# The second block's context weights move from SyncE's DMA queue to GpSimd's

## The chip, the cores and the metric

The kernel runs on one core of a Trainium2 chip. The metric is the device time of one execution in microseconds (us). The kernel before was timed three times; its time is the median of these runs.

## The reference

Two transformer blocks are computed in float32 for 512 latent tokens of width 1024; a sequence of 256 context tokens goes with each block. What matters here, cut short:

```
def reference(x, ..., ctx_2, ...):
    x = first_block(x, ...)      # differential attention + gated linear attention,
                                 # then 32 experts (2 per token, hidden width 512)
    return second_block(x, c_2, ctx_2, ...)   # DEPTH_2 = 2 layers

def second_block(x, c, ctx, ...):
    for i in range(2):
        last = i == 1
        hc = modulate(rms_norm(ctx), ...);  pc = hc @ w_in[i]   # context path
        k_na_c, v_na_c, k_mla_c, v_mla_c = ...                  # keys and values from pc
        h = modulate(rms_norm(x), ...);     p = h @ w_in[i]     # latent path
        y_na  = neighbourhood_attention(q, k, v, k_na_c, v_na_c, bias)
        y_gm  = spatial_gating(...)
        y_mla = dense_attention(q, [k_mla_c, k], [v_mla_c, v])
        x = x + g1 * merge_branches(y_na, y_gm, y_mla, gates, ...)
        x = x + g2 * (square(relu(h2 @ ffn_w1[i])) @ ffn_w2[i])
        if not last:  # the same three branches, merge and MLP for the context
            ctx = ctx + ...
    return x
```

The context path of layer 0 depends on nothing that the first block computes. In layer 1 it only makes keys and values.

## The kernel before

**Precision and weights.** Large products are made of three matmuls: each operand is split into a high part (fp32r) and a low part, and high by high, high by low and low by high are added up in PSUM (`mm3`, lines 188 to 194). Weights come from HBM as float32 in pieces of 128x1024 (512 KB). `load_split` (line 176) takes a `raw` buffer, loads a piece with `load` (line 151), and splits it with `split`: ScalarE writes the high part `wh` (line 168), VectorE the low part `wl` (line 169). There are four `raw` buffers and six `hl` buffers for the parts. A chunk of 256 output columns over a depth of 1024 is two pieces, so the raw buffers hold two chunks.

**Queues.** Every `load` is issued on SyncE (SP, line 152): the context's and the latent path's pieces (`wr`), the experts' weights (`we`, 384 pieces of 512 KB into 14 `wa` buffers, line 973), modulation weights and constants. GpSimd (POOL) issues the stores of results to HBM, the reading back of stored keys and values, the indirect gathers (token rows `xb` for the experts, line 979; expert results `yr`, line 1053) and the stores of expert results `Yd` (line 1041). It also computes: `acc` sums of `merge` (line 1732), sums of squares in `stat` (line 241), zeroing of `xb` (line 978).

**Order.** `weave` (line 79) writes the program out by the streams' planned times: the context path of layer 0, `path(0, 256)`, goes between the steps of the first block's output projection, routing, experts and combination (`run`, lines 401 to 411). Its MLP falls into the second half of the experts. The context path of layer 1, `path(1, 256)`, is woven into the MLP of layer 0's latent path (`self.fill`). That program order gives priorities; a planner then fixes each engine's queue when the kernel is built, taking what it holds ready, by priority. At run time every engine, SP and POOL too, takes its queue strictly in order: an instruction that waits holds all that stands behind it.

Experts go by in 16 pairs. A pair is 32 instructions each for gate and up (`gu`, line 1019) and 32 for down (`py`, line 1038), and its results go from PSUM to `yb` (ScalarE line 165, VectorE line 986) and by POOL to `Yd`.

Of the kernel before, what the change touches and what calls it, by code (L numbers as in the profile page):

```python
# [104 lines left out]
class Gen:  # L105
# [67 lines left out]
        self.nc.scalar.activation(hi, ps, AF.Copy, scale=g)  # L173
        self.nc.vector.scalar_tensor_tensor(lo, ps, g, hi.bitcast(F32), op0=OP.mult, op1=OP.subtract)

    def load_split(self, src, width):

        out = []
        total = src.shape[-1]
        for o in range(0, total, 1024):  # L180
            m = min(1024, total - o)
            raw = self.load(self.H.get("raw", self.nm("wr"))[:, :m], src[:, o:o + m])
            hi, lo = (self.H.get("hl", self.nm("w" + c), F32R)[:, :m] for c in "hl")
            self.split(hi, lo, raw)
            out += [(hi[:, j:j + width], lo[:, j:j + width]) for j in range(0, m, width)]
        return out
# [991 lines left out]
    def path(self, L, n, side=None, before=None):  # L1178
        nc, A = self.nc, self.A
        T = n // P  # L1180
        lat = n == 512
        kv_only = L == 1 and not lat
        src = self.xs_dram[L] if lat else (A["ctx2T"], self.xctx_dram)[L]
        dst = (self.xs_dram[1], self.out)[L] if lat else self.xctx_dram
        W = A["w_in2"][L]
        m = self.gains(L, 0 if lat else 1, 1)
# [17 lines left out]
        d = self.ctx_dram[L]  # L1204

        def row_tiles(chunk, evac, cols=256):
            w = self.load_split(W[chunk], 256)
            for t in range(T):
                ps = self.mm()
                self.rows(ps[:, :cols], h, t, [(x[:, :cols], y[:, :cols]) for x, y in w])  # L1210
                evac(t, ps[:, :cols])
                yield 2.6 if t == T - 1 else -2.6
# [30 lines left out]
        raw = yield from heads64(0, "k")  # L1243
# [48 lines left out]
        raw = yield from heads64(6, "q")  # L1292
# [57 lines left out]
        X = self.load_x(src, n, "xr")  # L1350
        ss = []
        for c in range(4):
            w = self.load_split(A["w_out2"][L, c], 256)
            for j in range(2):
                ps = self.mm()
                self.colsT(ps[:, :n], w, j, mg)
                i = 2 * c + j
                nc.vector.scalar_tensor_tensor(X[i], ps[:, :n], m["g1"][:, i:i + 1], X[i], op0=OP.mult, op1=OP.add)
                self.stat(ss, i, X[i], n)
                yield (5.1 if j else -5.1) * w1  # L1360
# [9 lines left out]
    def mlp(self, L, n, X, h2, g2, dst):  # L1370

        nc, A = self.nc, self.A
        w1, follow = n / 512, n == 512 and L == 0
        for q in range(4):
            u = self.pairs(8, n, "u")
            for c in range(4):
                w = self.load_split(A["ffn_w1"][L, q * 4 + c], 256)
                for j in range(2):
                    ps = self.mm()
                    self.colsT(ps[:, :n], w, j, h2)  # L1380
                    t = self.t2("uu")[:, :n]
                    nc.scalar.activation(t, ps[:, :n], AF.Relu)
                    nc.vector.tensor_tensor(t, t, t, op=OP.mult)
                    self.split(*u[2 * c + j], t)
                    yield (5.1 if j else -5.1) * w1
            if q == 3 and follow:
                ss = []
            for c in range(4):
                w = self.load_split(A["ffn_w2"][L, q, c], 256)
                for j in range(2):  # L1390
                    ps = self.mm()
                    self.colsT(ps[:, :n], w, j, u)
                    i = 2 * c + j
                    nc.vector.scalar_tensor_tensor(X[i], ps[:, :n], g2[:, i:i + 1], X[i], op0=OP.mult, op1=OP.add)
                    if q == 3:
                        nc.gpsimd.dma_start(dst[i], X[i])
                        if follow:
                            self.stat(ss, i, X[i], n)
                    yield (5.1 if j else -5.1) * w1
        if follow:  # L1400
            self.X, self.ss = X, ss
# [132 lines left out]
    def latent_attention(self, L, n, low, column, y):  # L1534
# [20 lines left out]

        for half in range(2):

            wkv = self.load_split(A["mla_w_ukv"][L, half], 512)
            KQ = [self.at("mkq") if lat else self.t2("mkr") for _ in range(T)]
            KR, VR = [x[:, :384] for x in KQ], self.many(T, 256, "mvr")  # L1560
            for t in range(T):
# [21 lines left out]
                    nc.gpsimd.dma_start(vc[t], d["vml"][t][:, half * 256:(half + 1) * 256])  # L1583
                vs = VR + vc
            if not kv_only:
                wq = self.load_split(A["mla_w_uq"][L, half], 384)
                QR = [KQ[t][:, 384:] if lat else self.t2("mqr") for t in range(T)]
                for t in range(T):
                    if t % 2 == 0:
                        room = self.dd("q")  # L1590
                    ps = room[:, t % 2 * 512:t % 2 * 512 + 384]
                    self.rows(ps, cq, t, wq)
                    self.copy_act(QR[t][:, :384], ps)
                yield 1
                r = rms(QR, 96)
                yield 1
                for t in range(T):
                    x = QR[t][:, :384].rearrange("p (h c) -> p h c", h=4)
                    tt(x, x, r[:, t][:, :, None].to_broadcast([P, 4, 96]), op=OP.mult)
                    x = x[:, :, 64:]  # L1600
                    if not lat:
                        tt(x, x, gq[:, 64:][:, None, :].to_broadcast([P, 4, 32]), op=OP.mult)
                        continue

                    tmp = self.t2("rp")
                    u, v = (tmp[:, i * P:(i + 1) * P].rearrange("p (h c) -> p h c", h=4) for i in range(2))
                    for o, z in ((u, rc), (v, rs)):
                        tt(o, x, z[:, t * 32:t * 32 + 32][:, None, :].to_broadcast([P, 4, 32]), op=OP.mult)
                    x, u, v = (z.rearrange("p h (a i c) -> p h a i c", a=2, i=2) for z in (x, u, v))
                    tt(x[:, :, :, 0], u[:, :, :, 0], v[:, :, :, 1], op=OP.subtract)  # L1610
                    tt(x[:, :, :, 1], u[:, :, :, 1], v[:, :, :, 0], op=OP.add)
                    yield 0.5
# [53 lines left out]
    def gating(self, L, n, h, W, row_tiles):  # L1666

        nc, A = self.nc, self.A
        T = n // P
        lng, lnb, ws, bs = (self.load(self.t2(x), A[x][L]) for x in ("gm_ln_g", "gm_ln_b", "gm_w_s", "gm_b_s"))  # L1670
        gv = [self.t2("gv") for _ in range(T)]
        sums = self.small(2 * T, "gsum")
        for c in range(2):
            def evac(t, ps):
                nc.scalar.activation(gv[t][:, c * 256:(c + 1) * 256], ps, AF.Gelu, accum_out=sums[:, c * T + t:c * T + t + 1])
            yield from row_tiles(8 + c, evac)
        mu, va = self.small(T, "gmu"), self.small(T, "gvs")
        nc.vector.tensor_tensor(mu, sums[:, :T], sums[:, T:], op=OP.add)
        nc.vector.tensor_scalar(mu, mu, -1.0 / 512, None, op0=OP.mult)
        for t in range(T):  # L1680
            sq = self.t2("sq")
            nc.scalar.activation(sq, gv[t], AF.Square, bias=mu[:, t:t + 1], accum_out=va[:, t:t + 1])
        rs = self.rsqrt(va, T, 1.0 / 512)
        for t in range(T):
            nc.vector.tensor_scalar(gv[t], gv[t], mu[:, t:t + 1], rs[:, t:t + 1], op0=OP.add, op1=OP.mult)
            nc.vector.tensor_tensor(gv[t], gv[t], lng, op=OP.mult)
            nc.vector.tensor_tensor(gv[t], gv[t], lnb, op=OP.add)
        u = self.many(4, n, "gu")
        for c in range(2):
            w = self.load_split(W[10 + c], 256)  # L1690
            for j in range(2):
                ps = self.mm()
                self.colsT(ps[:, :n], w, j, h)
                nc.scalar.activation(u[2 * c + j], ps[:, :n], AF.Gelu)
                yield (5.1 if j else -5.1) * T / 4
        y = self.pairs(4, n, "ygm")
        for g in range(4):
            ps = self.tp("gs")
            for t in range(T):
                nc.tensor.matmul(ps[:, t * P:(t + 1) * P], gv[t][:, g * P:(g + 1) * P], ws[:, g * P:(g + 1) * P], start=True, stop=True)  # L1700
            x = self.t2("gx")[:, :n]
            nc.vector.tensor_tensor(x.rearrange("p (t c) -> p t c", t=T), ps[:, :n].rearrange("p (t c) -> p t c", t=T),
                                    bs[:, g * P:(g + 1) * P][:, None, :].to_broadcast([P, T, P]), op=OP.add)
            nc.vector.tensor_tensor(x, x, u[g], op=OP.mult)
            self.split(*y[g], x)
        yield 1
        return y

    def merge(self, L, n, h, W, b, y, acc):
# [1 line left out]
        nc, A = self.nc, self.A  # L1711
        wo = A[("na_w_o", "gm_w_o", "mla_w_o")[b]][L]
        for c in range(4):
            w = self.load_split(W[12 + b * 4 + c], 256)
            th = []
            for j in range(2):
                ps = self.mm("pg")
# [3 lines left out]
                yield (5.1 if j else -5.1) * n / 512  # L1721
            if callable(y):
                y = y()
            w = self.load_split(wo[c], 256)
            for j in range(2):
                i = 2 * c + j
                ps = self.mm("pp")
# [170 lines left out]
```

## Time and profile before

| | us |
|---|---|
| median of three runs | 3545.32 |
| lowest and highest | 3538.56, 3549.27 |
| the profiled execution, its own time | 3544.75 |
| its span in the trace | 3542.7 |
| granted TensorE clock, mean share of full speed | 0.973 |

The span runs from the first to the last instruction in the trace; the profiled execution's own time is 2.05 us longer. Times in rows are counted from the span's start. PE is TensorE's matmuls, PEld its weight loads, DVE VectorE, ACT ScalarE, POOL GpSimd; SPq is the queue in which SyncE issues. A matmul's end is modelled, so a busy PE isn't one at its peak.

### The profile page before, as it was taken

To read this page: it belongs to the slowest core of one execution; us is meant where nothing else is said; L and a number is where in the kernel's file an instruction comes from. 1 tells how busy PE (TensorE), PEld (TensorE's weight loads), DVE (VectorE), ACT (ScalarE), POOL (GpSimd) and SP (SyncE) were. 2 spreads that over 40 slices of the span, in tenths; PEclk is the share of its full clock that TensorE was granted. 3 is DMA by queue.
4 is the path that set the end of the run, shared out by engine and by line. 5 is a ranking of instruction groups with operands and counts; after the bars stand their busy time and mean duration, and the time that the engine had idled before them with its cause. 6 is when DMAs were issued, how large, how long until landed. Compare 5 with 4: busy or idle time off the path is not lost. (4 is left out here: it accounts for less than half of the span.)

```text
span 3542.7 us, 48935 instructions
## 1 busy us (share of the span) xinstructions
PE 3357.0 (95%) x19280; PEld 2533.0 (71%) x19280; DVE 1693.2 (48%) x3173; ACT 1234.2 (35%) x2194; POOL 340.3 (10%) x410
## 2 busy tenths in 40 slices
PE   7999998999999999699999999999999999999999
PEld 4987546665666666497577777888797777778887
DVE  5336545435333333454347755444654466644443
ACT  4214314334322322233344433333334444423222
POOL 1000011012111100400001011000300001020000
PEclk9999999999999999799999999999999999999999
DMA  7241567898899898534642132333433221132332
GB/s 262 88 128 36 189 213 259 317 360 329 309 358 352 305 358 320 205 92 137 226 144 68 56 98 96 106 117 114 152 96 105 78 71 59 49 113 86 100 99 79
DMA packets 197459, 596.03 MB, mean 168 GB/s; under 512 B 32123, under 2 KB 36987, under 8 KB 197228
## 3 DMA queue, kind: packets, MB, share of 16 engines
q1 hardware_dynamic: 178460, 539.65, 43.8%
q0 software_dynamic: 18768, 53.24, 4.2%
q8 instruction: 152, 2.49, 0.3%
q14 instruction: 79, 0.65, 0.1%
HBM read 563.69 MB, written 33.29 MB: 169 GB/s over the span
## 5 line engine op out<-in xcount | busy, mean ns | idle before, releaser
L169 DVE TENSOR_TENSOR wl<-wr,wh 128x1024 fp32r<-128x1024 f32 (+2 forms) x452 | 553.0, 1229 | 534.3 <-ACT wh L168 504.6
L168 ACT ACTIVATE wh<-wr 128x1024 fp32r<-128x1024 f32 (+2 forms) x452 | 471.1, 1047 | 697.5 <-PE mm L193 489.8
L192 PE MATMUL mm<-wh,h 128*128 128x256 f32 (+1 forms) x1104 | 322.5, 292 | 6.3 <-ACT h L277 4.6
L193 PE MATMUL mm<-wl,h 128*128 128x256 f32 (+1 forms) x1104 | 318.8, 289 | 0.0
L194 PE MATMUL mm<-wh,h 128*128 128x256 f32 (+1 forms) x1104 | 318.0, 289 | 0.3 <-DVE h L278 0.2
L192 PE MATMUL mm<-u,wh 128*128 128x512 f32 (+1 forms) x768 | 276.6, 361 | 10.8 <-ACT wh L168 10.8
L192 PE MATMUL mm<-f,wh 128*128 128x512 f32 (+1 forms) x768 | 275.2, 361 | 8.6 <-ACT wh L168 5.0
L194 PE MATMUL mm<-u,wl 128*128 128x512 f32 (+1 forms) x768 | 274.3, 359 | 2.9 <-DVE wl L169 2.9
L193 PE MATMUL mm<-f,wh 128*128 128x512 f32 (+1 forms) x768 | 274.3, 358 | 0.0
L194 PE MATMUL mm<-f,wl 128*128 128x512 f32 (+1 forms) x768 | 273.3, 358 | 1.0 <-DVE wl L169 1.0
L193 PE MATMUL mm<-u,wh 128*128 128x512 f32 (+1 forms) x768 | 274.1, 358 | 0.0
L1019 PE MATMUL gu<-we,xT 128*64 128x512 f32 x1024 | 251.7, 601 | 0.7 <-ACT xT L165 0.7
L192 PEld LDWEIGHTS mm<-wh,h 128*128 128x128 f32 x1104 | 217.2, 197 | 20.1 <-issue 9.0
L194 PEld LDWEIGHTS mm<-wh,h 128*128 128x128 f32 x1104 | 216.3, 196 | 6.8 <-issue 4.7
L192 PE MATMUL pg<-h,wh 128*128 128x512 f32 (+1 forms) x576 | 213.0, 370 | 7.3 <-ACT th L1720 4.2
L193 PEld LDWEIGHTS mm<-wl,h 128*128 128x128 f32 x1104 | 217.3, 197 | 3.0 <-issue 2.3
L193 PE MATMUL pg<-h,wh 128*128 128x512 f32 (+1 forms) x576 | 208.4, 362 | 0.0
L194 PE MATMUL pg<-h,wl 128*128 128x512 f32 (+1 forms) x576 | 208.4, 362 | 0.0
L355 ACT ACTIVATE p<-S,mx 128x768 f32<-128x768 f32 (+2 forms) x192 | 144.7, 756 | 104.4 <-DVE mx L1427 61.9
L192 PEld LDWEIGHTS mm<-u,wh 128*128 128x128 f32 x768 | 147.8, 192 | 46.3 <-ACT wh L168 15.8
L192 PEld LDWEIGHTS mm<-f,wh 128*128 128x128 f32 x768 | 147.3, 192 | 41.8 <-issue 8.1
L194 PEld LDWEIGHTS mm<-u,wl 128*128 128x128 f32 x768 | 147.4, 193 | 25.5 <-DVE wl L169 4.7
(505 smaller groups left out, 6390.2 us busy)
## 6 DMA issues: line engine op xcount, KB each, us to landing
wr<-in_ffn_w_dram SPq DMA_DIRECT2D x192, 512.0 KB, 3.7
wr<-in_w_in_dram SPq DMA_DIRECT2D x178, 512.0 KB, 4.5
we<-in_expert_w_gate_dram SPq DMA_DIRECT2D x128, 512.0 KB, 8.3
we<-in_expert_w_up_dram SPq DMA_DIRECT2D x128, 512.0 KB, 9.7
we<-in_expert_w_down_dram SPq DMA_DIRECT2D x128, 512.0 KB, 8.4
wm<-in_w_mod_dram SPq DMA_DIRECT2D x96, 256.0 KB, 5.9
wm<-in_w_mod_dram SPq DMA_DIRECT2D x48, 512.0 KB, 4.9
wm<-in_w_ada_dram SPq DMA_DIRECT2D x64, 256.0 KB, 4.9
```

What stands on the lines that cost most here:

```text
L168: self.nc.scalar.activation(hi, src, AF.Copy)
L169: self.nc.vector.tensor_tensor(lo, src, hi.bitcast(F32), op=OP.subtract)
L192: mm(out, ah, bh, start=i == 0, stop=False)
L193: mm(out, ah, bl, start=False, stop=False)
L194: mm(out, al, bh, start=False, stop=i == n - 1)
L355: self.nc.scalar.activation(p, s, AF.Exp, bias=m, accum_out=sm)
L1019: nc.tensor.matmul(gu[64 * e:64 * e + 64, m * 512:m * 512 + 512], xT[k // 4][:, o:o + 64], w[e][kk], start=k == 0, stop=k == KD - 1)
```

## The change

`load_split` gets an argument that names the queue. The context path passes GpSimd's, the latent path and all else keep SyncE's: `lat` is true, and `n` is 512, for the latent path. Of the 452 pieces that `load_split` loads, 148 move: 136 of `path(0, 256)` (48 of `w_in2`, 12 of the three `w_o`, 8 of `w_out2`, 64 of the MLP, 2 of `mla_w_ukv`, 2 of `mla_w_uq`) and 12 of `path(1, 256)`. Buffers, splits, matmuls and the program's order are as before.

```diff
-    def load_split(self, src, width):
+    def load_split(self, src, width, queue=None):
...
-            raw = self.load(self.H.get("raw", self.nm("wr"))[:, :m], src[:, o:o + m])
+            raw = self.H.get("raw", self.nm("wr"))[:, :m]
+            (queue or self.nc.sync).dma_start(raw, src[:, o:o + m])
...
         def row_tiles(chunk, evac, cols=256):
-            w = self.load_split(W[chunk], 256)
+            w = self.load_split(W[chunk], 256, None if lat else nc.gpsimd)
...
-            w = self.load_split(A["w_out2"][L, c], 256)
+            w = self.load_split(A["w_out2"][L, c], 256, None if lat else nc.gpsimd)
...
         w1, follow = n / 512, n == 512 and L == 0
+        queue = nc.sync if n == 512 else nc.gpsimd
...
-                w = self.load_split(A["ffn_w1"][L, q * 4 + c], 256)
+                w = self.load_split(A["ffn_w1"][L, q * 4 + c], 256, queue)
...
-                w = self.load_split(A["ffn_w2"][L, q, c], 256)
+                w = self.load_split(A["ffn_w2"][L, q, c], 256, queue)
...
-            wkv = self.load_split(A["mla_w_ukv"][L, half], 512)
+            wkv = self.load_split(A["mla_w_ukv"][L, half], 512, None if lat else nc.gpsimd)
...
-                wq = self.load_split(A["mla_w_uq"][L, half], 384)
+                wq = self.load_split(A["mla_w_uq"][L, half], 384, None if lat else nc.gpsimd)
...
-            w = self.load_split(W[10 + c], 256)
+            w = self.load_split(W[10 + c], 256, nc.sync if n == 512 else nc.gpsimd)
...
-            w = self.load_split(W[12 + b * 4 + c], 256)
+            queue = nc.sync if n == 512 else nc.gpsimd
+            w = self.load_split(W[12 + b * 4 + c], 256, queue)
...
-            w = self.load_split(wo[c], 256)
+            w = self.load_split(wo[c], 256, queue)
```

## Rows read from the trace of the kernel before

**Rows 1.** The page's first part: busy us, share of the span, instructions.
```profile
PE 3357.0 (95%) x19280; PEld 2533.0 (71%) x19280; DVE 1693.2 (48%) x3173; ACT 1234.2 (35%) x2194; POOL 340.3 (10%) x410
```
**Rows 2.** Busy time by stretch: length, each engine's us, then PE clock, DMA share, GB/s.
```profile
480.00:620.00 140.00, 127.74 (x671) 80.76 (x671) 74.01 (x208) 46.86 (x75) 27.00 (x36) 0.95 0.70 245
620.00:1043.00 423.00, 417.30 (x2576) 264.99 (x2574) 169.73 (x379) 147.31 (x311) 62.53 (x90) 1.00 0.90 336
1043.00:1440.00 397.00, 375.31 (x2216) 239.49 (x2212) 130.61 (x200) 106.80 (x169) 30.36 (x41) 0.97 0.87 326
1440.00:1520.00 80.00, 44.33 (x252) 39.88 (x252) 47.62 (x81) 22.16 (x27) 35.11 (x40) 0.68 0.48 171
...
2225.00:2530.00 305.00, 304.84 (x1464) 256.33 (x1463) 146.15 (x216) 106.14 (x152) 15.56 (x26) 1.00 0.36 114
```
**Rows 3.** What SP waited for, 1043 to 1440 us: total us, times, longest.
```profile
SPq L152 <- DVE wl L169: 107.2, 27, 13.0
SPq L152 <- PE gu L1019: 66.9, 23, 8.5
```
**Rows 4.** What PE waited for, 1043 to 1440 us, same columns.
```profile
PE mm L192 <- ACT wh L168: 13.6, 9, 1.7
...
PE mm L194 <- DVE wl L169: 3.0, 6, 0.5
```
**Rows 5.** The pieces wr, 1043 to 1440 us: waits on them; issue to landing.
```profile
  ACT wh L168: 18.2, 4
...
DMA to landing us min/median/max: 3.6/7.0/11.7
```
**Rows 6.** Timelines of ACT and PE around one stall: start, us, what, [idle before <-releaser].
```profile
1260.99 0.60 ACT L1024 ACTIVATE hT<-gu 128x512 f32<-128x512 f32 x1 [13.35 <-PE gu L1019]
1261.48 2.00 ACT L168 ACTIVATE wh<-wr 128x1024 fp32r<-128x1024 f32 x2
...
1253.83 7.09 PE L1019 MATMUL gu<-we,xT 128*64 128x512 f32 x32
1262.58 0.39 PE L192 MATMUL mm<-u,wh 128*128 128x256 f32 x1 [1.67 <-ACT wh L168]
```
**Rows 7.** Timeline of SP ahead of that stall.
```profile
1239.63 10.49 SPq L152 DMA_DIRECT2D wr<-in_ffn_w_dram  x4
```
**Rows 8.** Issue durations in ns (min/median/max), by line of issue.
```profile
L152 SPq DMA_DIRECT2D wr<-in_ffn_w_dram x192: 327/328/740, 1043.4 to 3503.6; - x192
L1041 POOL DMA_DIRECT2D Yd<-yb x32: 539/576/609, 659.8 to 1440.7; - x32
```
**Rows 9.** Timeline of POOL after one pair of experts.
```profile
713.54 0.61 POOL L1041 DMA_DIRECT2D Yd<-yb  x1 [48.83 <-ACT yb L165]
...
717.40 1.03 POOL L979 DMA_INDIRECT xb<-Hd,cc  x1 [0.27 <-POOL xb L978]
```
**Rows 10.** What POOL waited for, 1043 to 1440 us.
```profile
POOL Yd L1041 <- ACT yb L165: 319.0, 8, 50.7
```
**Rows 11.** PE alone in two stretches after a stall: length, busy (instructions), clock, DMA, GB/s.
```profile
1442.00:1445.50 3.50, 3.50 (x17) 0.53 0.79 241
1445.50:1450.00 4.50, 4.50 (x39) 0.98 0.70 250
```
**Rows 12.** Timeline of POOL during the routing.
```profile
563.27 0.54 POOL L828 DMA_DIRECT2D Hd<-h2r  x1 [41.15 <-ACT h2r L165]
...
580.26 1.01 POOL L978 MEMSET xb<- 128x512 f32 x2
584.30 0.54 POOL L828 DMA_DIRECT2D Hd<-h2r  x1 [3.03 <-ACT h2r L165]
```
**Rows 13.** Timelines of SP and POOL at the experts' end.
```profile
1441.93 1.47 SPq L152 DMA_DIRECT2D wr<-in_ffn_w_dram  x2
...
1448.59 1.01 POOL L1053 DMA_INDIRECT yr<-Yd,cc  x1 [0.65 <-DMA wr<-in_ffn_w_dram]
```
**Rows 14.** The page's groups: busy us, mean ns of one, idle before.
```profile
L169 DVE TENSOR_TENSOR wl<-wr,wh 128x1024 fp32r<-128x1024 f32 (+2 forms) x452 | 553.0, 1229 | 534.3 <-ACT wh L168 504.6
```

## The prediction

> **What bounds the kernel now.** I read the page's shares of busy time first, then the busy times by stretch, then who waits for whom, and the timelines last. PE is busy 95% of the span, POOL 10% [rows 1]. Averages hide stages, so the table by stretch decides [rows 2]. The 136 pieces of `path(0, 256)` run beside routing (480 to 620 us), the experts with the context's attention (620 to 1043), the experts with its MLP (1043 to 1440) and the combination (1440 to 1520); the other 12 run beside the latent MLP (2225 to 2530). PE is idle for 140 − 127.7 = 12.3 us, 423 − 417.3 = 5.7, 397 − 375.3 = 21.7, 80 − 44.3 = 35.7 and 305 − 304.8 = 0.2 us in these. So TensorE sets the pace wherever the moved loads stand. The transfers run at up to 336 GB/s there, a second and close limit, but not the one that ends last.
>
> SP, the queue that the change relieves, stands waiting for most of the MLP stretch: 107.2 us for raw buffers that VectorE's split must free, 66.9 us for expert buffers that `gu` must free [rows 3]. Each wait holds the other stream's loads. But in that stretch PE lost only 13.6 us, 9 times, to a high part and 3.0 us to a low part [rows 4], and only 4 splits on ACT waited for their piece, 18.2 us in all [rows 5].
>
> What such a PE stall is shows in one of them [rows 6, 7]. PE ends `gu` at 1253.83 + 7.09 = 1260.92 us; ACT then does `hT` (0.60 us), and only behind it the splits `wh` (2.00 us for two). PE waits 1.67 us, which is 0.60 and 1.07 for the first split, and no transfer. The four pieces before it were issued from 1239.63 us on, within 10.49 us; with 7.0 us to landing [rows 5] they were there by 1257.1 us, over 4 us before the split. ACT's order made the stall, not SP's.
>
> **The change part by part.**
>
> *What SP is relieved of.* 148 issues at 0.328 us [rows 8] are 48.5 us of issuing, and the waits of [rows 3]. Expert loads may go up to 13.0 us earlier (the longest wait for a raw buffer). No row of [rows 4] is a PE wait for an expert's weights, and their buffers are freed by PE itself. Gain on the path: 0. The cover is the 14 buffers of expert weights.
>
> *When a context piece can go.* It needs a raw buffer, which is freed by a split, which needs an `hl` buffer, which PE frees. None of this changes. On POOL it no longer waits behind expert loads, but it gets no buffer earlier. Gain from earlier landing: at least 0, at most all of what PE lost to splits in the MLP stretch, 13.6 + 3.0 = 16.6 us, and the clock that went with it: the stretch ran at 0.97, so 0.03 x 397 = 11.9 us. The top is 28.5 us. The planner might place splits ahead of `hT` if it sees pieces land earlier; as the stall that I followed had its piece in time, I take a third of the 16.6 us without the clock: −5.5 us.
>
> *What POOL issues.* 148 issues at 0.576 us, the nearest row being `Yd` stores [rows 8], are 85 us more on an engine that is busy 10% of the time: hidden. The piece is larger than those stores (512 against 256 KB), so the cost of one issue is bounded by 0.539 below and, for twice the bytes at twice the longest, 1.22 us above; I take 0.576, as both have 128 rows. If POOL had no slack, 136 x 0.576 = 78 us would show.
>
> *What a piece is queued behind.* POOL waits in order, up to 50.7 us, for `yb` of a pair of experts [rows 10], and then issues `Yd`, zeroes and gathers from 713.54 to 717.40 + 1.03 = 718.43 us, 4.9 us [rows 9]. A piece planned behind this lands 7.0 us later [rows 5] and is split in 1.07: 13.0 us after `yb`. Its cover is two chunks of raw buffers: a chunk is 48 matmuls (two halves of eight depths, three products each) at 4.50/39 = 0.115 us [rows 11], 5.5 us, so 11.1 us for two, and with one stretch of 32 expert matmuls (7.09 us, [rows 6]) 18.2 us. Cost per pair: 13.0 − 18.2, that is nothing, to 13.0 − 11.1 = 1.9 us; if the cover were gone, 13.0 us. I take 0, as expert matmuls stand between the chunks. The planner isn't bound to program order: the experts' zeroing of `xb` ran ahead of two of the routing's stores [rows 12], so a load that is ready can stand ahead of a `Yd` that isn't.
>
> *What is queued behind a piece.* A piece that waits for a raw buffer now holds POOL: the gathers for the next pair, which have the rest of a pair of some 50 us (the 50.7 us in [rows 10]) as cover, and at the end the last `Yd`, on which the eight gathers `yr` depend. Two context pieces were still to come at 1441.93 us, beside gathers from 1448.59 us on [rows 13]. On POOL they cost 2 x 0.576 = 1.2 us of issue and, ahead in its queue, up to 2 x 512 KB at 326 GB/s [rows 2], 3.2 us. They shared the transfer engines already, so I take +1.5 us between 0 and +4.4.
>
> *The 12 pieces of layer 1.* PE has no idle time beside them (304.84 of 305 us), so they can only lose; the latent MLP's matmuls cover a late one. I take 0, bounded by 12 x 1.9 = 23 us.
>
> Sum: −5.5 + 1.5 = −4.0 us on the profiled execution's 3544.75, which is 0.57 below the median: 3541 us.
>
> **A rule that speaks against the change.** In [rows 8] 32 issues from POOL took 539 to 609 ns, so nothing held one by more than 70 ns. The Trainium skill, SBUF — State Buffer (section "SBUF: two separate sides"), says that VectorE in a two-port mode keeps GpSimd from writing the descriptors of its own DMAs, and that SyncE's DMAs are immune. By the rows the sum has nothing for it; by the rule context pieces could be delayed wherever VectorE copies or scales in SBUF. It is the fourth case below.
>
> **The rivals.**
>
> 1. *No change that can be measured* (forecast): the relief is off PE's path, POOL's slack holds the issues. For it: [rows 4, 5]. 3541 us.
> 2. *Faster*: the planner, no longer seeing context pieces behind expert loads, puts splits ahead of `hT` and `yb`, and the stalls go with their clock. 3544.75 − 28.5 = 3516 us. For it: in [rows 6] PE did no context matmul during the 7.09 us of `gu`, so `hl` buffers for the split can have been free that long. Against: its pieces were in time anyhow. It decides from 4 of the 9 stalls on, at 28.5/9 = 3.2 us each.
> 3. *Slower, by POOL's order*: pieces stand behind `Yd` and the gathers and come late. With 1.9 us at each of 16 pairs, and for each stall 1.5 us of half clock (17 matmuls at 0.206 in place of 0.115 us, [rows 11]): 16 x 3.4 = 54 us at most; half of it gives 3572 us. For it: POOL waits 319.0 us at eight `Yd` [rows 10], and 41.15 us at one `Hd` store [rows 12]. Against: planner order and two chunks of cover. It decides as soon as a piece is needed within 13 us after `yb`.
> 4. *Slower, by VectorE holding POOL's descriptors*: an issue held for one of VectorE's commonest instructions, the split, comes 1.23 us late [rows 14]. Covered in nine loads of ten, that leaves 14 stalls at 1.23 us and 1.5 us of half clock, +38 us: 3583 us. Against: [rows 8], where none of 32 issues was held.
>
> That the change does nothing at all isn't among them: the loads do move; that it has no effect on the time is case 1.
>
> **How the numbers follow.** Case 1 gets 0.42, case 2 gets 0.31, case 3 gets 0.22, case 4 gets 0.05. The planner makes every engine's order anew, so case 1 has its own scatter: within 0.3% (10.6 us, what a measurement of this kernel can tell from no change) of 3545. The range reaches below to case 2 with the idle clock of the routing stretch too (0.05 x 140 = 7 us): 3545 − 28.5 − 7 = 3509, and above to case 3 with the middle of the layer 1 bound: 3572 + 11 = 3583. Case 1 alone: 3534 to 3555. Faster 0.31, same 0.42, slower 0.27.
>
> **What would show it.** In the changed kernel SP's waits for VectorE's split vanish in 620 to 1440 us, and POOL has 148 `wr` issues near 0.58 us. Right: PE idle in 620 to 1440 us stays within 10 us of 27.4, and the waits for `wh` keep their 1.67 us shape. Case 2: these waits shrink below 8 us and the clock there reaches 1.00. Case 3: PE waits for `wh` of many us, with ACT waiting for a `wr` issued by POOL right behind a `Yd`. Case 4: POOL issues of over 1 us. Wrong altogether, if the end of the experts near 1440 us moves with no change in these waits.

## The result and the profile after

The changed kernel takes 3501.94 us (median, 3498.14 to 3509.37) against 3542.24 us for the kernel before (its three runs and a fourth): ratio 0.9887, 95% interval 0.9873 to 0.9900. It is faster by 1.1%, and lies below the predicted range. The profiled execution took 3501.3 us, its span is 3499.5.

The page's first part for the kernel after answers to [rows 1]:

```profile
PE 3328.7 (95%) x19280; PEld 2520.3 (72%) x19280; DVE 1692.5 (48%) x3173; ACT 1235.7 (35%) x2194; POOL 420.9 (12%) x558
```

The table by stretch answers to [rows 2], but is cut at the same events in both kernels: first `gu`, start of the context's MLP (first `ss`), end of the last `py`, last `rb` of the combination, end. Columns: stretch, length, busy us of PE, PEld, DVE, ACT, POOL, then PE clock, DMA share, GB/s. After:

```profile
615.26:1046.78 431.52, 424.70 (x2603) 267.04 (x2603) 175.00 (x384) 152.32 (x317) 99.78 (x155) 0.99 0.91 340
1046.78:1394.94 348.16, 343.43 (x2206) 229.90 (x2204) 130.57 (x199) 108.06 (x167) 60.42 (x97) 0.99 0.97 366
1394.94:1462.89 67.95, 34.19 (x204) 30.88 (x204) 36.69 (x65) 15.92 (x19) 35.54 (x40) 0.68 0.49 174
1462.89:3499.50 2036.61, 1955.59 (x10964) 1591.75 (x10964) 1050.17 (x1816) 767.15 (x1348) 154.64 (x178) 0.98 0.32 101
```

The same cuts in the kernel before:

```profile
616.87:1047.53 430.66, 424.96 (x2603) 267.28 (x2603) 172.45 (x381) 149.63 (x314) 62.53 (x90) 0.99 0.90 336
1047.53:1439.06 391.53, 370.78 (x2196) 238.19 (x2194) 130.34 (x199) 105.90 (x167) 30.36 (x40) 0.97 0.87 328
1439.06:1510.36 71.30, 36.49 (x213) 32.98 (x213) 39.37 (x68) 18.98 (x22) 35.11 (x40) 0.69 0.54 192
```

The gain is one stretch: the context's MLP beside the experts is 43.4 us shorter, the combination 3.4, the experts beside attention 0.9 longer, and the rest, to the end, 4.3 longer (2032.34 before). Inside the 43.4 us, PE's idle time fell from 391.53 − 370.78 = 20.8 to 4.7 us (16.0 of it), and 27.4 us are *busy* time. By line (count | busy us, mean ns), the expert matmuls of that stretch, before and after:

```profile
L1019 PE MATMUL gu<-we,xT 128*64 128x512 f32 x450 | 111.8, 598 | 0.0
...
L1038 PE MATMUL py<-we,hT 128*64 128x512 f32 x256 | 64.7, 609 | 0.0
```

```profile
L1020 PE MATMUL gu<-we,xT 128*64 128x512 f32 x450 | 99.8, 595 | 0.0
...
L1039 PE MATMUL py<-we,hT 128*64 128x512 f32 x256 | 59.3, 606 | 0.1
```

The same 706 records take 17.4 us less, with at most 0.1 us of idle time ahead of them in either kernel. A table of waits can't show this, and the mean hardly does, as matmuls overlap. The remaining 10 us are mostly the context's matmuls, for two reasons: a granted clock of 0.99 in place of 0.97, which is worth 0.03 x 391.5 − 0.01 x 348.2 = 8 us at most over all matmuls, and the context's side of the cuts that the next section shows.

The waits of SP and PE after, 1046 to 1395 us, answer to [rows 3] and [rows 4]:

```profile
SPq L152 <- PE gu L1020: 159.6, 55, 12.9
SPq L152 <- PE py L1039: 89.4, 32, 12.3
...
SPq L183 <- DVE wl L169: 4.3, 1, 4.3
```

```profile
PE rb L209 <- DVE rs L222: 3.5, 1, 3.5
PE xt L209 <- ACT hT L165: 0.7, 1, 0.7
```

SP now waits for the experts' own buffers, so their loads run as early as 14 buffers allow, and all nine stalls of PE for `wh` are gone. POOL's queue answers to [rows 8] and [rows 10]: issues (ns min/median/max) and waits:

```profile
L183 POOL DMA_DIRECT2D wr<-in_ffn_w_dram x64: 537/540/592, 1009.1 to 1387.4; - x64
L183 POOL DMA_DIRECT2D wr<-in_w_in_dram x58: 537/548/599, 455.2 to 2366.5; - x58
```

```profile
POOL wr L183 <- DVE wl L169: 195.5, 47, 11.0
POOL Yd L1042 <- ACT yb L165: 72.9, 7, 22.7
```

### The profile page after: what moved, and what is told of

Read it like the earlier page. It is cut to its first block, busy times and chain, and to the rows that moved or that the text cites. A ratio compares the mean times of both kernels' runs of the same rounds, so it can differ in the third digit from the quotient of the medians.

```text
span 3499.5 us, 48890 instructions
## 1 busy us (share of the span) xinstructions
PE 3328.7 (95%) x19280; PEld 2520.3 (72%) x19280; DVE 1692.5 (48%) x3173; ACT 1235.7 (35%) x2194; POOL 420.9 (12%) x558
## 5 line engine op out<-in xcount | busy, mean ns | idle before, releaser
L168 ACT ACTIVATE wh<-wr 128x1024 fp32r<-128x1024 f32 (+2 forms) x452 | 473.8, 1049 | 723.5 <-PE mm L194 546.6
L1020 PE MATMUL gu<-we,xT 128*64 128x512 f32 x1024 | 239.4, 599 | 0.2 <-ACT xT L165 0.2
L1020 PEld LDWEIGHTS gu<-we,xT 128*64 128x64 f32 x1024 | 71.4, 137 | 129.1 <-issue 121.4
```

The costliest lines, as they stand in the source:

```text
L168: self.nc.scalar.activation(hi, src, AF.Copy)
L1020: nc.tensor.matmul(gu[64 * e:64 * e + 64, m * 512:m * 512 + 512], xT[k // 4][:, o:o + 64], w[e][kk], start=k == 0, stop=k == KD - 1)
```

## What a cut in an expert block costs

A block (all of a pair's `gu` for gate or up, or its `py`) is 16 matmuls; the trace writes two records for each, so the 32 "instructions" of a block are 32 records. The two experts of a pair alternate and use 64 columns of the array each. Where PE's order puts context matmuls inside a block, the block falls into runs. From the timeline of PE in the kernel before (start, us, what, records):

```profile
1127.10 5.37 PE L1019 MATMUL gu<-we,xT 128*64 128x512 f32 x24
...
1132.71 1.07 PE L1019 MATMUL gu<-we,xT 128*64 128x512 f32 x2
1133.71 0.38 PE L193 MATMUL mm<-u,wh 128*128 128x256 f32 x1
...
1134.29 0.28 PE L194 MATMUL mm<-u,wl 128*128 128x256 f32 x1
1134.41 0.28 PE L192 MATMUL mm<-u,wh 128*128 128x256 f32 x1
1134.62 1.93 PE L1019 MATMUL gu<-we,xT 128*64 128x512 f32 x6
1136.48 0.39 PE L193 MATMUL mm<-u,wh 128*128 128x256 f32 x1
1136.70 0.28 PE L194 MATMUL mm<-u,wl 128*128 128x256 f32 x1
```

Twelve matmuls took 5.37 us, one took 1.07, three took 1.93; whole blocks of 16 take 7.09 [rows 6]. That is 0.43 us for each matmul, plus 0.2 us a run, plus **0.43 us where the number is odd**: one takes as long as two (4 records took 1.08 us elsewhere), three as long as four (8 records, 1.94). A couple, one matmul of each expert, takes its 0.86 us side by side; a matmul whose partner is cut off uses that time alone. As ends are modelled, the starts are the better witness, and they agree: from its start to the next context matmul's, the single one took 1.00 us and the three took 1.86. The context pays at a cut too: its matmuls start 0.12 us apart, but 0.21 us ahead of a run and 0.22 behind it. The Trainium skill, TensorE: Matmul & The Clock Gate (section "Part 3: Packing small matmuls — row/col tiling"), says that small matmuls in different tiles of the array run concurrently; these rows agree, and show what it costs when the order parts them.

In TensorE's planned order the kernel before has 94 runs, 46 of an odd number; the changed kernel has 70 and 18. In the MLP stretch 21 of its 22 blocks are whole, against 11 of 22. 0.43 x 28 + 0.2 x 24 = 16.8 us; measured over both expert stretches 373.0 − 355.4 = 17.6 us.

## The experiments

All medians with the ratio to the kernel before, timed beside it on the same chip (its medians there were 3541.7 to 3543.9 us). "Last `rb`" is when the combination ends; "runs" are those in TensorE's order. "wh" is PE's idle time for the split's high part and "SP wl" SP's wait for the split, both in each kernel's own MLP stretch.

| kernel | median, us | ratio [95%] | last `rb` | runs (odd) | expert matmuls, us | wh, us | SP wl, us |
|---|---|---|---|---|---|---|---|
| before | 3542.2 | | 1510.4 | 94 (46) | 373.0 | 13.6 | 107.2 |
| after | 3501.9 | 0.9887 [.9873, .9900] | 1462.9 | 70 (18) | 355.4 | 0 | 4.3 |
| mlp_only | 3507.5 | 0.9902 [.9882, .9921] | 1466.3 | 70 (18) | 357.8 | 0 | 4.5 |
| all_but_mlp | 3518.7 | 0.9935 [.9915, .9954] | 1484.6 | 79 (28) | 361.7 | 4.4 | 65.1 |
| experts_pool | 3508.8 | 0.9905 [.9886, .9923] | 1466.2 | 70 (18) | 356.8 | 0 | 296.3 |
| before_whole | 3492.8 | 0.9851 [.9829, .9873] | 1459.8 | 69 (0) | 349.7 | 0 | 11.3 |
| before_even | 3503.6 | 0.9883 [.9865, .9901] | 1470.2 | 89 (0) | 352.4 | 0 | 80.6 |
| after_even | 3498.8 | 0.9877 [.9860, .9893] | 1458.4 | 70 (0) | 350.0 | 0 | 3.9 |
| after_frag | 3511.1 | 0.9912 [.9895, .9928] | 1470.8 | 132 (24) | 370.9 | 0 | 1.9 |
| after_odd | 3518.4 | 0.9928 [.9912, .9945] | 1480.2 | 137 (36) | 376.0 | 0 | 0.4 |
| before_n44 | 3541.5 | 0.9990 [.9979, 1.0001] | 1501.7 | 81 (30) | 361.3 | 11.7 | 85.6 |
| before_n40 | 3547.1 | 1.0009 [.9999, 1.0020] | 1515.2 | 104 (60) | 380.2 | 22.2 | 127.6 |
| after_n40 | 3488.5 | 0.9838 [.9821, .9854] | 1448.9 | 76 (24) | 357.6 | 0 | 0 |
| after_whole | 3508.5 | 0.9892 [.9872, .9911] | 1472.7 | 70 (0) | 355.4 | 0 | 4.5 |
| before_r2w16 | 3630.6 | 1.0251 [1.0233, 1.0268] | 1544.7 | 107 (58) | 383.2 | 17.6 | 135.8 |
| after_r2w16 | 3618.3 | 1.0223 [1.0201, 1.0244] | 1524.1 | 69 (18) | 368.1 | 7.6 | 0 |
| before_even_n40 | 3498.1 | 0.9877 [.9860, .9894] | 1458.5 | 94 (0) | 351.1 | 3.1 | 98.5 |
| after_even_n40 | **3477.6** | 0.9820 [.9802, .9837] | 1437.6 | 75 (0) | 347.1 | 0 | 0 |

### Which loads, and which queue

**mlp_only**: the diff's edit in the MLP's loads alone.

```
         queue = nc.sync if n == 512 else nc.gpsimd   # w1 and w2 of the MLP
...
         w = self.load_split(W[chunk], 256)           # the other callers as before
```

> Only the loads of the context MLP (w1 and w2 of both layers where the rows are the context's) go to GpSimd's queue; projections, gates and output weights stay on SyncE's with the experts. Theory 1 (SyncE's queue serves in order, so a wait for a raw buffer there holds the expert weights behind it, and the order of TensorE's work has expert blocks cut into fragments among context matmuls; both queues apart, blocks stay whole): the whole gain lies in the context MLP stage, so -36 to -46 us against the kernel before, 3496 to 3506 us, and the last py ends near 1395 us. Theory 2 (context splits land earlier and leave their place behind hT and yb on ScalarE, the stalls and their clock are all): the same stage, so also near -40, but with the fragments still there. Rival, chance of a new plan: any value within +-20 us of the kernel before.

**all_but_mlp**: the complement, `queue = nc.sync` in the MLP and the diff's edit everywhere else.

> The counterpart: every context load but those of the context MLP goes to GpSimd's queue. Theory 1: the MLP's raw buffers still share SyncE's queue with the experts, but the planned order has some 9 extra fragments of expert blocks in place of 24, so 10 to 25 us less than the kernel before, with PE waits for wh of 1.67 us remaining in part. Theory 2 alone (no fragments in the argument): within 0.3% of the kernel before, the stalls stay as they were. Chance of a new plan: any value within +-20 us.

**experts_pool**: the kernel before with the *experts'* loads moved.

```
-        w = self.load(self.wa("we"), self.A["expert_w_" + m][e, q])
+        w = self.wa("we")
+        self.nc.gpsimd.dma_start(w, self.A["expert_w_" + m][e, q])
```

> The mirror image of the change: the experts' weights go to GpSimd's queue, every context load stays on SyncE's. Theory 1 (it is the separation that counts, not which queue the context is on): expert blocks whole again, -30 to -45 us, less what expert loads lose behind Yd and the gathers of GpSimd. A rival (what counts is that GpSimd's queue, idle, issues context pieces early): expert loads behind Yd come late instead, PE waits for we of several us at each of 16 blocks of pairs, same as before or slower by up to 50 us.

The MLP's loads alone bring 34 of the 40 us, the others 23, so the two halves overlap; by theory 2 the others should have brought nothing. And the mirror image brings 33 us: which queue carries the context matters little, that the two streams are apart counts. There SP still waits for the split far longer than in the kernel before, and little is lost by it, as only context loads stand behind; the experts' loads on POOL wait for their own buffers. From the waits of SP and POOL in experts_pool, 1049 to 1398 us:

```profile
SPq L152 <- DVE wl L169: 296.3, 42, 28.8
```

```profile
POOL we L969 <- PE gu L1020: 91.5, 44, 9.6
POOL we L969 <- PE py L1039: 66.0, 16, 11.6
```

### The order of TensorE with both streams on one queue

**before_whole**: no load is moved. A block's eight weights are taken first and used last-loaded first, so its matmuls are ready together.

```
-                for q in range(4):
-                    w = [self.weights() for _ in range(2)]
-                    for kk in range(2):
+                ws = [[self.weights() for _ in range(2)] for _ in range(4)]
+                for q in reversed(range(4)):
+                    w = ws[q]
+                    for kk in reversed(range(2)):
...
-                        for e in range(2):
+                        for e in reversed(range(2)):
```

> The kernel before with both of its loads on SyncE's queue; only the experts' loop is changed: all eight weight pieces of a block are taken first and used last-taken first, so that the matmuls of one block can't be cut apart by the arrival of a piece. If fragments are the larger part of the loss (theory 1): the expert matmuls' busy time in the context MLP stage falls by some 15 us from 176, and the kernel gains 15 to 30 us while the stalls for wh may stay. If only the stalls behind hT and yb and their clock count (theory 2): within 0.3% of the kernel before. If the shared queue makes weights late whatever the order (theory 3): waits of TensorE for we appear, and the kernel is slower by 10 us or more.

**before_even**: no load is moved. Only the two experts of a couple change places, so that a couple's first matmul needs the weight loaded last.

```
-                        for e in range(2):
+                        for e in (1, 0):
```

> The kernel before, all loads on SyncE's queue; in the experts' loops only the order of the two experts of a pair is turned (second first), so that the first matmul of a couple waits for the weight that is loaded last. Expert blocks are still cut into nearly as many runs (89 planned in place of 94), but no cut falls between the two experts of a couple. Theory A (a cut costs because it parts the two 64-column matmuls of a couple, 0.43 us each time: gu x2 took 0.65 or 1.07 us, x6 1.51 or 1.93): some 45 parted runs in the trace of before, so -19 us, 3523 us or less. Theory B (the number of cuts costs, by the switch between context and expert matmuls): 5 of 24 extra cuts fewer, -5 to -10 us. Theory C (weights and pieces late by SyncE's order, whatever the cuts look like): within 0.3% of the kernel before.

**after_even**: the same line in the changed kernel.

> The changed kernel with the same turn of the two experts in a couple: 70 planned runs of expert matmuls as in the changed kernel, none of them parting a couple. The trace after has 17 runs with a parted couple, all ahead of the context MLP. Theory A: -7 us against the changed kernel, 3495 us, all of it between 616 and 1047 us. Theory B: no change against it.

Both kernels on SyncE's queue alone gain about what the change gained, or more: 49 and 39 us, where 15 to 30 and 19 were expected. before_even still cuts its blocks (89 runs), none odd, and has lost the stalls too. after_even took 3 us off the changed kernel (7 were expected), and its expert matmuls 5.4. So the loss in the kernel before goes with an order that parts couples; as the turn removed the stalls together with the parted couples, these runs don't separate the two. (The 0.65 and 1.51 us in before_even's expectation are not whole runs: a whole run of two records takes 1.07 us and one of six 1.93, as above.)

The timelines suggest why the stalls went. After `gu`, ACT and VectorE need some us before PE gets `ht`, and PE fills them with context matmuls that are ready. Context matmuls (`mm`) between the end of `gu` and `ht`, in the kernel before (the stall of [rows 6]), after, and before_even (length, PE busy (records), clock, DMA share, GB/s):

```profile
1260.92:1264.00 3.08, 0.74 (x4) 1.00 0.86 344
```

```profile
1235.60:1244.30 8.70, 8.70 (x72) 1.00 1.03 416
```

```profile
1234.36:1244.00 9.64, 9.08 (x72) 1.00 1.00 363
```

The kernel before has four context matmuls for this place and waits for the split behind `hT` at the first; the other two have 72. In the changed kernel ACT has its splits done 6 us ahead of `hT`, and the next one waits for PE to free a buffer; but in before_even the split still runs right behind `hT`, as in the kernel before, without a stall (timelines of ACT, after and before_even):

```profile
1235.73 0.60 ACT L1025 ACTIVATE hT<-gu 128x512 f32<-128x512 f32 x1 [6.11 <-PE gu L1020]
1240.09 1.06 ACT L168 ACTIVATE wh<-wr 128x1024 fp32r<-128x1024 f32 x1 [3.76 <-PE mm L194]
```

```profile
1234.36 0.60 ACT L1024 ACTIVATE hT<-gu 128x512 f32<-128x512 f32 x1 [9.50 <-PE gu L1019]
1234.86 2.00 ACT L168 ACTIVATE wh<-wr 128x1024 fp32r<-128x1024 f32 x2
```

So it seems to be a stock of context matmuls that keeps PE from stalling, which the kernel before has used up as filling inside its cut blocks. That reading is argued from these three places; no run changed the stock alone.

### Cuts made by hand in the changed kernel

**after_frag** and **after_odd**: `yield 4.2` after a gate or up block is replaced by cuts between couples, or inside one.

```
-                yield 4.2
+                    yield 1.05                # after_frag: after each quarter
...
+                            if kk and not e:  # after_odd: after the first expert
+                                yield 1.05
```

> The changed kernel, gate and up blocks cut by hand at every quarter (a yield of 1.05 after each couple of weights in place of 4.2 after the block): 132 planned runs in place of 70, the added cuts between couples. Theory A: only the switch itself costs, 0.2 us on the expert's side (x2 0.65 us is 0.43 + 0.2) and about as much on the context's: 62 x 0.2 to 0.4 = +12 to +25 us against the changed kernel. Theory B (each cut costs what the 24 extra cuts of before cost, 27 us beside its stalls, 1.1 us each): +70 us. Theory C (loads apart, cuts are harmless): within 0.3% of the changed kernel.

> The changed kernel cut by hand as often as in the other run of this kind (137 planned runs), but in the midst of a couple: the yield stands after the first expert's matmul of the second half of each quarter. Theory A: 64 such cuts part a couple at 0.43 us each beyond what the cuts between couples cost, +27 us against that run, +40 to +50 us against the changed kernel, with expert runs of odd and parted length in the trace. Theory B: the same time as the run with cuts between couples. Theory C: within 0.3% of the changed kernel.

62 more runs cost 9.2 us, below theory A's 12 to 25 and far from B's 70: 0.15 us each. after_odd costs 7.3 us more than after_frag, where +27 was expected, and 16 us more than the changed kernel, where 40 to 50 were. The size was wrong because most of its runs start inside a couple but have an even number, and couple up with the next matmul of the other expert: only 36 are odd against 24, which is 0.43 x 12 + 0.2 x 5 = 6.2 us. Measured in the expert matmuls: 376.0 − 370.9 = 5.1 us.

### Is it one lucky order?

**before_n44**, **before_n40**, **after_n40**: the number with which an expert block enters the planning of the order, 4.2, becomes 4.4 or 4.0.

```
-                yield 4.2
+                yield 4.4
...
-            yield 4.2
+            yield 4.4
```

> The kernel before with one number of the order's planning turned: the work that an expert block is said to stand for is 4.4 us in place of 4.2. Nothing else is changed, all loads stay on SyncE's queue. The planned order of TensorE has 81 runs of expert matmuls in place of 94, 30 of them of an odd number in place of 46 (the changed kernel: 70 and 18). Theory A (a run costs 0.2 us and, with an odd number, 0.43 us more): expert matmuls 9.5 us shorter; with the stalls that go with the cuts, as in the run without the MLP's loads on GpSimd, -10 to -23 us, 3519 to 3532 us. Rival (what counts is which queue carries the loads): within 0.3% of the kernel before.

> The same number turned the other way, 4.0 in place of 4.2, all loads on SyncE's queue: 104 planned runs, 60 of an odd number. Theory A: expert matmuls 8 us longer than in the kernel before, 381 in place of 373 us, and the kernel +8 to +18 us, 3550 to 3560 us. Rival (queue alone): within 0.3% of the kernel before.

> The changed kernel with the same 4.0 in place of 4.2: 76 planned runs, 24 of an odd number, in place of 70 and 18. Theory A: +4 us, 3502 to 3510 us. If the changed kernel's gain were a lucky plan and not the separation of the queues, this plan should lose most of it: 3530 us or more, as the kernel before does with either number.

**after_whole**: before_whole's edit in the changed kernel.

> The changed kernel with the experts' eight weights taken first and used last first, as in the run of the kernel before of that kind: 70 planned runs, none odd. It has in the same order both what the queues and what whole blocks bring. If both bring the same thing (no parted couples, no cuts in the MLP stage): within 0.3% of that run, 3488 to 3498 us. If the separated queue brings something of its own beside the order: 3480 us or less.

Theory A alone fell here. before_n44's expert matmuls are 11.7 us shorter, and its median is the same within its interval. Its stalls stayed, seven in the MLP stretch (PE's waits):

```profile
PE mm L192 <- ACT wh L168: 11.7, 7, 1.7
```

And it ran out of context work sooner: in the combination PE waited 13.06 us at once for a gathered row (timeline of PE, the number in brackets). The profiled execution still ended its combination 8.7 us sooner; why the median of ten runs shows 2 us of that stays open.

```profile
1450.71 0.69 PE L208 MATMUL yT<-cc,yr 128*128 128x128 f32 x2 [13.06 <-DVE yr L1056]
```

So runs and their odd numbers explain the length of the expert matmuls (0.43 us for each of 768, and 0.2 and 0.43 us for runs and odd numbers as above, give 2 to 6 us less than measured; after_whole and the two kernels with two raw buffers, below, are 7 to 16 us above), and not the whole time. before_n40 lost less than theory A said (3.6 us, not 8 to 18), and after_n40 gained 13 us where A had it lose 4. Separating the queues holds in the second plan too, where it brought more: 3547.1 to 3488.5. after_whole went the other way, 16 us slower than before_whole, against both of its expectations; before the MLP stretch TensorE waited there for weights, 3.55 us at the longest (timeline of PE). Why its plan came out worse stays open.

```profile
820.55 1.98 PE L1021 MATMUL gu<-we,xT 128*64 128x512 f32 x4 [3.55 <-DMA we<-in_expert_w_up_dram]
```

### Is it the wait at the head of SyncE's queue?

**before_r2w16**, **after_r2w16**: two raw buffers fewer, two weight buffers more.

```
-T2, WA, RAW, HL, AT = 35, 14, 4, 6, 9
+T2, WA, RAW, HL, AT = 35, 16, 2, 6, 9
```

> The kernel before with two raw buffers in place of four, and the two given to the expert weights (16 in place of 14; the sum of the buffers stays). All loads on SyncE's queue. If the wait for a raw buffer at the head of that queue is what costs: SyncE's waits for the split's low half in the context MLP stage grow beyond the 107 us of before, more and longer stalls of TensorE for wh, +15 us or more, 3557 us and up. If expert weights only lack buffers (the rival): faster than before, by up to the 13 us that a weight buffer more for each expert would give back; by the plan alone (107 planned runs, 58 of an odd number): +8 us.

> The changed kernel with the same two raw and sixteen weight buffers; context loads on GpSimd's queue. If the wait at the head of the shared queue is what costs, raw buffers are nothing to the experts here: within 10 us of the changed kernel, 3492 to 3512 us. If the changed kernel's gain needs the depth of raw buffers (context pieces landing early): +15 us or more, as on the shared queue.

**before_even_n40**, **after_even_n40**: turned couples with 4.0.

> The kernel before on SyncE's queue alone, with the couples turned (second expert first) and 4.0 in place of 4.2: another plan with 94 runs, none of an odd number. If the turn itself cures the shared queue: near the run with 4.2, 3495 to 3512 us, without stalls of TensorE for wh behind hT. If that run was one lucky plan: stalls are back, 3525 us or more (the kernel before with 4.0 was at 3547).

> The changed kernel with the couples turned and 4.0: 75 planned runs, none odd. The turn took 3 us off the changed kernel, and 4.0 took 13: if they add up, 3484 to 3488 us. If the separate queue is worth nothing once couples are turned: the same as the other kernel of this kind on SyncE's queue, within 10 us.

The wait by itself is not the cost. With two raw buffers SP's wait did grow, to 135.8 us, but both kernels lose, the separated one as well (+116 us against the changed kernel, where 10 were allowed; up to the last `rb` 61 us, against 34 on the shared queue): so raw buffers seem to be needed for their own sake, though the edit moved two buffers and the plan with them. And before_even_n40 is 46 us faster than the kernel before beside it, as its expectation for a cure had it, with nearly as long a wait of SP for the split (98.5 us in a stretch of 338, against 107.2 [rows 3] in 392), while before_n44 gained nothing with a shorter one, 85.6. SP's waits of before_even_n40 in its MLP stretch:

```profile
SPq L152 <- DVE wl L169: 98.5, 23, 8.6
```

The medians by queue and by couples:

| | couples as before, 4.2 | 4.0 | couples turned, 4.2 | 4.0 |
|---|---|---|---|---|
| one queue | 3542.2 | 3547.1 | 3503.6 | 3498.1 |
| two queues | 3501.9 | 3488.5 | 3498.8 | 3477.6 |

Two queues bring 40 and 59 us where couples can be parted, 5 and 20 where they can't. The two edits mostly remove the same loss; what the second queue keeps of its own is the smaller part, and it varies with the plan: with whole blocks it cost 16 us. Both edits with 4.0 give the fastest kernel tried, 6 us below what was expected if the gains added up. Its MLP stretch (columns as in the table by stretch) has next to no idle time:

```profile
1048.87:1365.46 316.59, 315.94 (x2020) 207.61 (x2018) 120.18 (x184) 97.45 (x149) 56.63 (x90) 1.00 0.98 375
```

## Why the prediction was wrong

- **"What SP is relieved of … Gain on the path: 0" failed.** Its reason was that no row of [rows 4] is a PE wait for an expert's weights. That is true: over the whole run PE and PEld idled 6.1 us ahead of the expert matmuls for a weight's transfer, and 1.6 after. But the order of TensorE is fixed ahead of the run, and with both streams on one queue it begins blocks with half a couple and fills the gap with context matmuls. The loss stood in the busy column: 17.6 us of expert matmuls. No term of the sum could hold it.
- **"Gain from earlier landing … −5.5 us" was mis-sized.** The stalls are all gone: 16.0 us of idle time and at most 8 us of clock in the MLP stretch. This is near rival 2's size (16.6 and 11.9), and its marks showed: waits for `wh` below 8 us, clock near 1.00. Its mechanism, splits ahead of `hT`, is there in the changed kernel but not in before_even, which lost the stalls as well; what both have is a stock of matmuls. With the matmuls' 17.6 us rival 2's 3516 us would be 3499, against the profiled 3501.3; that this is so close is in part luck, as rival 2 had too much for the clock and nothing for the context's side of the cuts.
- **POOL's issue hidden, nothing behind `Yd`: right.** 148 issues of 537 to 599 ns left PE no new wait in the MLP stretch, and their pieces landed there in 6.8 us (median; 7.3 before), so rivals 3 and 4 are out. The rule of the Trainium skill that was weighed there (SBUF — State Buffer, "SBUF: two separate sides") showed no sign in these issues and landings.
- **Combination +1.5:** measured −3.4 us; the two context pieces that stood beside the gathers [rows 13] are issued by 1387.4 us, which fits, but no run tried this alone. **Layer 1's pieces 0:** the rest is 4.3 us longer in one execution, inside the bound of 23.
- The sign "wrong altogether, if the end of the experts moves with no change in these waits" didn't come: the end moved by 44 us and the waits went with it.

## What to carry to other kernels

Two load streams with different buffers on one in-order queue shape the whole planned order, also where no engine is ever seen waiting for a late load; so ask what the order will look like with each stream running as far ahead as its own buffers allow. Where matmuls run in couples, compare their busy time divided by their count between stretches (111.8 and 99.8 us for 450), and not the mean of one (598 and 595 ns): it shows parted couples that no table of waits shows. A one-line turn, needing the last-loaded operand first, gained nearly as much as the queue; both together, with 4.0, gained 1.8%.

## What was not expected of the hardware

A 64-column matmul without its partner took the couple's time: 1.07 us for one, 1.08 for two. With two streams apart, transfers reached a share of 0.97 to 0.98 (366 to 375 GB/s) in the MLP stretch against 0.87 (328). It is nearly the same load in less time (127.52 MB against 128.29 before), so this follows from the shorter stretch and didn't cause it; before_whole, on one queue, had 371 GB/s. The Trainium skill, DMA: Bandwidth & Descriptors (section "Issuing engines are not separate DMA queues"), says that issuing from several engines saves only the time of issue. That time wasn't what the change gained here: SP stood waiting for buffers for 174 us of the MLP stretch before (107.2 and 66.9 [rows 3]) and for 249 after.
